# A hybrid attention and S5 layer on one core: gate spills moved to ScalarE's queue, own buffers for scaled u, output transposes and gate tiles moved in the state-space loop, the attention gate scaled ahead of its product

## Chip, cores and metric

The kernel runs on one core of a Trainium2 chip. Its engines are TensorE (PE), VectorE (V, in the trace DVE), ScalarE (A, ACT), GpSimd (Q, POOL) and SyncE (SP), which only issues DMAs here. The metric is the device time of one execution in microseconds, the median of the runs.

## What is computed

One layer over 1024 tokens of width 1024, in float32:

```python
xn = rms_norm(h, mix_norm)
q, k, v, gate_a, u, gate_s = split(xn @ w_in)          # 512 columns each
attn = dilated_mixture_attention(q, k, v, q_norm, k_norm) * silu(gate_a)   # 8 heads of 64
ssm  = s5_glu(u, ...) * silu(gate_s)                   # 32 groups of 16 channels, 64 complex states
h = h + concat(attn, ssm) @ w_out
h = h + sigmoid(rms_norm(h, ple_norm) @ w_ple_gate) * (p @ w_ple_proj)
```

The state-space part is a linear recurrence per group, `x[t] = a x[t-1] + B u[t]`, `y = Re(C x) + D u`, then a GELU and a gated linear unit.

## The kernel before

Each large product is made of three passes on PE (`mm3`): both factors are split into a high part and a residue, written `wh`, `wl` and `xh`, `xl`. A weight tile of 128 by 512 comes by DMA into one of three raw buffers (`wr`), ScalarE makes `wh` of it (L177), and POOL or VectorE the residue `wl` (L178). A tile of the gates takes 24 matmuls.

The order of the work is the Tile scheduler's: every engine and SP's DMA queue has its own in-order list of instructions, sorted by program order, by the priorities that `tc.high_priority` gives, and by a simulated timeline. While `T.held` is true, PE's instructions stay in the order in which the program writes them; that is so from the first gate tiles to the end of the state-space loop. The q, k, v products behind it are free again.

The stages that the change touches:

- **u and its scaling.** First u is computed for all tokens (tile by tile into PSUM, copied by ScalarE to `uraw`, L243 and L251). The gate tiles need the two "big" banks that the last copies of u (L251) free. `stats_rows` (L204) makes the row factor `rrow`. Then L496 to L507 multiply u by `rrow` on POOL (e = 0) and VectorE (e = 1) into eight tiles `ust`, which SP stores to `u_s` in DRAM; `ssm_inputs` loads them back as `ut` in another layout. The `ust` tiles come from `ev`, a ring of four buffers, which the gate tiles (`gate_a`, `gate_s`) use too. The pool `s2`, which holds the scan's tiles, is opened after the pool of `uraw` is closed (L509, L510) and lies over its memory.
- **The gates.** `gates()` (L282) is a generator: one step computes a tile of the attention gate (eight tiles, the first two together, so seven steps) or of the state-space gate (eight steps), applies SiLU on ScalarE, and SP stores it to `sa_s` or `sg_s` (L289, L299). `fill(n)` takes n steps. There is one step before the parameters, three at L495, one between `kern_pe(0)` and `kern_pe(1)`, one in each iteration of the loop, and one more in iterations 0 and 1 (L685). So the loop has a gate tile in iterations 0 to 7.
- **The parameters.** VectorE works out the powers of the recurrence (`pa`, `pb`, `mcs`, `msn`); four of their rows are copied by ScalarE at L487 to L490.
- **The state-space loop** has nine iterations, for half u blocks i = 0 to 7. Iteration i does on PE: `scan_pe(i)` (vp), `fill`, `ssm_out(i-1)` (yp), in iterations 2, 4, 6, 8 `ssm_store` (yt: transposes of the gelu of yp, which ScalarE makes at L643), and `kern_pe(i+2)` (gp, a transpose of the kernel `g`, and kp). Beside it VectorE and POOL do the scan (L613 to L625), the kernel of i + 2 (`kern_build`) and the tables of i + 1 (`table`). gp and yt use the "t" banks, of which there are two; ScalarE copies yt out at L653 (yo) and gp at L553. The scan's scratch tiles are in a ring of `SB[7]` buffers.
- **Attention** (L795) runs block by block, woven into the v, GLU and output products by `step(n)`. For each head: scores, row minimum, exp, split into f16 halves (L846 to L851), a transposing DMA to `pt`, and pv, which is summed in the one "pv" bank. Then pv is multiplied by the factor of the softmax sum, `dn` (L876). `output(b)` (L798) loads the gate tile into one buffer, POOL multiplies by it (L802), and PE transposes the product. The outputs of blocks 0, 1, 4 and 5 are held back to a later block.

Of the kernel before, what the change touches and what calls it, by code (L numbers as in the profile page):

```python
# [10 lines left out]
F32 = mybir.dt.float32  # L11
# [4 lines left out]
OP = mybir.AluOpType  # L16
# [41 lines left out]
VG = ((0, 1), (2,), (3,), (4,), (5,), (6,), (7,))  # L58
OS = (2,) * 8 + (3,) * 8
PB = {"prb": (2, 2), "hl": (2, 2), "pt": (3, 2)}  # L60
SB = (2, 1, 1, 1, 4, 4, 4, 8)
P = 128
S = 1024
D = 1024
# [17 lines left out]
def hybrid_layer(ctx: ExitStack, tc: tile.TileContext, a: dict, dbg=None):  # L82
# [199 lines left out]
    def gates():  # L282
        w = [load_w(wp, a["w_in"], k, 1536, lo=GLA) for k in range(KT)]
        for bs in ((0, 1), (2,), (3,), (4,), (5,), (6,), (7,)):
            for b, o in zip(bs, tok_tiles(w, bs, [f"ga{b}" for b in bs], "big")):
                gt_ = ev(f"gate_a{b}")
                with tc.high_priority(offset=AHEAD):
                    A.activation(gt_, o, AF.Silu, scale=rcol[:, b:b + 1])
                nc.sync.dma_start(sa_s[b], gt_)  # L289
            yield  # L290
        w = [load_w(wp, a["w_in"], k, 2560, lo=GL) for k in range(KT)]
        for f in range(4):
            for n in range(2):
                o = feat_tile(w, f, n, "big", f"gs{f}{n}")
                gt_ = ev(f"gate_s{f}{n}")
                with tc.high_priority(offset=AHEAD):
                    V.tensor_tensor(gt_, o, rrow[:, n * 512:(n + 1) * 512], op=OP.mult)
                    A.activation(gt_, gt_, AF.Silu)
                nc.sync.dma_start(sg_s[f * P:(f + 1) * P, n * 512:(n + 1) * 512], gt_)  # L299
                yield  # L300

    gates_ = gates()
# [181 lines left out]
    for j, m in enumerate((1, 2, 4)):  # L484
        turned(va[:, :, 0:m], vb[:, :, 0:m], va[:, :, m:2 * m], vb[:, :, m:2 * m], 3 * j, 3, [P, 3, m, G])
    turned(*(x[:, a_:a_ + 8].unsqueeze(1) for a_ in (18, 26) for x in (pa, pb)), 10, 1, [P, 1, 8, G])
    A.activation(pa[0:64, 8], mcs[0:64, 9], AF.Copy)  # L487
    A.activation(pa[64:128, 8], msn[64:128, 9], AF.Copy, scale=-1.0)
    A.activation(pb[0:64, 8], msn[0:64, 9], AF.Copy, scale=-1.0)
    A.activation(pb[64:128, 8], mcs[64:128, 9], AF.Copy, scale=-1.0)  # L490

    def rows(x, i, n, gs):
        return x[:, i:i + n, gs].rearrange("p i g -> p g i")

    fill(3)  # L495
    for f in range(4):  # L496
        ust = [ev(f"ust{f}{e}", (P, 4, P)) for e in range(2)]
        for n in range(2):
            o = uraw[f][:, n * 512:(n + 1) * 512]
            v5 = "p (b c e h) -> p e c b h"  # L500
            ov, rv = (t_.rearrange(v5, b=4, c=4, e=2) for t_ in (o, rrow[:, n * 512:(n + 1) * 512]))
            for e in range(2):
              with tc.high_priority(offset=AHEAD):
                E[UE[e]].tensor_tensor(ust[e][:, :, n * 64:(n + 1) * 64].rearrange("p c (b h) -> p c b h", b=4),
                                ov[:, e], rv[:, e], op=OP.mult)
        for e in range(2):
            nc.sync.dma_start(u_s[f, 4 * e:4 * e + 4].rearrange("j p k -> p j k"), ust[e])  # L507
# [151 lines left out]
    gcp = {i: kern_build(i) for i in range(2)}  # L659
    tabs = {0: table(0)}  # L660
    inp = {0: ssm_inputs(0)}
    gt = {0: kern_pe(0, *gcp[0])}
    fill()
    gt[1] = kern_pe(1, *gcp[1])
    for i in range(9):
        if i < 8:
            f = i // 2
            if i % 2 == 0 and f < 3:
                inp[f + 1] = ssm_inputs(f + 1)
            vp3 = scan_pe(i, gt[i], inp[f])  # L670
        fill()
        if i < 8:
            xpv[i] = ssm_scan(i, vp3, *tabs[i], gcp[i][1])
        if i + 2 < 8:
            gcp[i + 2] = kern_build(i + 2)
        if i + 1 < 8:
            tabs[i + 1] = table(i + 1)
        if i:
            f, h2 = divmod(i - 1, 2)
            if not h2:  # L680
                ygt[f] = [wa(f"ygt{f}{e}", (P, 4, 8, 16)) for e in range(2)]
            ssm_out(f, h2, xpv[i - 1], ygt[f], gcp[i - 1][1], inp[f], wts[f])
            if h2:
                ssm_store(f, ygt[f])
        if i < 2:  # L685
            fill()
        if i + 2 < 8:
            gt[i + 2] = kern_pe(i + 2, *gcp[i + 2])
    fill(16)
    T.held = False  # L690
    sp.close()

    rrp.close()
# [101 lines left out]
    def attention():  # L795
        held = []

        def output(b):  # L798
            n, at_ = b // 4, atok.pop(b)
            gl = b3[0].tile([P, 4, P], F32, tag="ga", name=f"ga{b}", bufs=GA)  # L800
            nc.sync.dma_start(gl, sa_s[b].rearrange("p (r t) -> p r t", r=4))
            E[EA[b % 2]].tensor_tensor(at_, at_, gl, op=OP.mult)  # L802
            tp = bank("t", f"at{b}").rearrange("p (r t) -> p r t", t=P)
            for j in range(4):
                T.transpose(tp[:, j], at_[:, j], ident)
            if n not in ma:
                ma[n] = quad(f"mah{n}"), quad(f"mal{n}")
            split(*(t_[:, b % 4] for t_ in ma[n]), tp.rearrange("p r t -> p (r t)"), V)

        atok = {}  # L810
        for i_, b in enumerate(BO):
            k0, k1 = dense_kb[b]
            n, nf = k1 - k0, int(b >= 4)
# [6 lines left out]
            def row_min(hd, out, sc, msk, init, acc_):  # L820
                V.tensor_tensor_reduce(out, sc, msk, gm, init, op0=OP.add, op1=OP.min, accum_out=acc_[:, hd:hd + 1])  # L821

            for h0 in range(0, H, m):
                pr_ = buf("prb", f"p{b}{h0}", (P, 5, P))
                sc = bank("s", f"sc{b}{h0}")
                if b == 7 and h0 % 4 == 0:
                    far7 = bank(F7, f"far{b}{h0}")
                    for j in range(4):
                        far_scores(far7[:, j * P:(j + 1) * P], b, h0 + j)
                elif nf and b < 7:  # L830
                    far_scores(sc[:, n * P:nt * P], b, h0)
                for i in range(m):
                    for qq, st_ in ((qh, True), (ql, False)):
                        T.matmul(sc[:, i * n * P:(i + 1) * n * P], qq[:, h0 + i, b * P:(b + 1) * P],
                                 ks[:, h0 + i, k0 * P:k1 * P], start=st_, stop=not st_)
                if nf:
                    far = far7[:, h0 % 4 * P:(h0 % 4 + 1) * P] if b == 7 else sc[:, n * P:nt * P]
                    row_min(h0, pr_[:, 0], far, mfar(b), 3.3e38, mf)
                for i in range(m):
                    hc = slice(h0 + i, h0 + i + 1)  # L840
                    pb_ = pr_[:, i * nt:(i + 1) * nt]
                    row_min(h0 + i, pb_[:, nf:nt].rearrange("p a b -> p (a b)"), sc[:, i * n * P:(i + 1) * n * P],
                            mdense(n - 1, n), mf[:, hc] if nf else 3.3e38, mx)
                    A.activation(pb_, pb_, AF.Exp, bias=mx[:, hc], scale=-1.0, accum_out=dn[:, hc])  # L844
                na = m * nt
                hl = halves(f"hl{b}{h0}")  # L846
                if HE[b][h0 % len(HE[b])] == "A":
                    A.activation(hl[:, 0:na], pr_[:, 0:na], AF.Copy)  # L848
                else:
                    V.tensor_copy(hl[:, 0:na], pr_[:, 0:na])  # L850
                E[LE[b][h0 % len(LE[b])]].tensor_tensor(hl[:, na:2 * na], pr_[:, 0:na], hl[:, 0:na], op=OP.subtract)  # L851
                pt = buf("pt", f"pt{b}{h0}", (P, 10, P), F16)
                nc.sync.dma_start(pt[:, 0:2 * na], hl[:, 0:2 * na], transpose=True)
                for i in range(m):
                    hd = h0 + i
                    end = hd == H - 1
                    for j in range(n):
                        for lp, lv in ((0, 0), (0, 1), (1, 0)):
                            T.matmul(pv[:, hd], pt[:, nf + i * nt + j + na * lp, :], vv[:, k0 + j, hd, lv, :],
                                     start=first, stop=end and not nf and j == n - 1 and lp == 1)  # L860
                            first = False
                    if nf:
                        for lp, lv in ((0, 0), (0, 1), (1, 0)):
                            for c in range(4):
                                T.matmul(pv[32 * c:32 * c + 32, hd], pt[:, na * lp, 32 * c:32 * c + 32],
                                         vc[:, c, hd, lv, :], start=False, stop=end and lp == 1,
                                         tile_position=(0, 32 * c))
                if h0 + m < H:
                    yield
# [2 lines left out]
                    output(b_)  # L872
            V.reciprocal(dn, dn)
            ts(dn, dn, isv, OP.mult)
            atok[b] = wa(f"atok{b}", (P, 4, P))
            tt(atok[b].rearrange("p r (h d) -> p (r h) d", d=64), pv, dn.unsqueeze(2).to_broadcast([P, 8, 64]), OP.mult)  # L876
            if i_ not in HOLD:
                output(b)
            yield
# [288 lines left out]
```

## Time and profile before

| | us |
|---|---|
| median of 3 runs | 720.25 (720.01 to 724.09) |
| the profiled execution, its own time | 726.85 |
| its span, first to last instruction | 725.1 |
| PE busy in it | 652.3 (90%) |
| VectorE, POOL, ScalarE busy | 434.9, 302.0, 299.0 |

Times in the profile are microseconds from the start of the span. A busy time counts instructions in execution; waits show as idle time before an instruction, with the engine or DMA that ended them. The granted clock is the share of the 2.4 GHz that PE was given: 1 is 2.4 GHz, 0.5 is 1.2 GHz. An `SPq` line is an instruction of SP's DMA queue, a `DMA` line the transfer.

### The profile page before, as it was taken

The numbers are of one execution on the slowest core, as the hardware profiler recorded it, in microseconds if no ns is written. First come the engines' busy times: TensorE is split into PE (matmuls) and PEld (weight loads), VectorE is DVE, ScalarE is ACT, GpSimd is POOL, SyncE is SP. The second block draws the span as 40 slices with busy tenths as digits, with TensorE's granted clock in tenths as the row PEclk, the third lists the DMA queues.
The fourth block names the chain that finished last, engine by engine and source line by source line (L and its number), as shares of the span: only waits on it lengthen the run. The fifth ranks groups of instructions, "written<-read, shape, count | busy, mean of one in ns | idle before, by whom it ended". The sixth has DMA issues, their size and how long they took to land.

```text
span 725.1 us, 11010 instructions
## 1 busy us (share of the span) xinstructions
PE 652.3 (90%) x3964; PEld 515.3 (71%) x3964; DVE 434.9 (60%) x904; ACT 299.0 (41%) x571; POOL 302.0 (42%) x263
## 2 busy tenths in 40 slices
PE   8996938997977999999999789888989899999997
PEld 6874826786866988887767366655767688888786
DVE  5999347573632546767553999967823565726222
ACT  7533105455556523346643655634512455203110
POOL 3435046664744411524242874422411325543531
PEclk9998977998989899999999889989989899999999
DMA  7712161415061765853672886699866334113201
GB/s 258 219 43 74 45 183 42 144 66 101 23 103 42 135 82 88 195 95 90 165 128 61 204 184 142 167 203 202 167 170 205 127 117 131 59 59 122 81 29 59
DMA packets 155047, 87.26 MB, mean 120 GB/s; under 512 B 117232, under 2 KB 126320, under 8 KB 154992
## 3 DMA queue, kind: packets, MB, share of 16 engines
q1 hardware_dynamic: 154992, 86.56, 49.2%
q8 instruction: 31, 0.51, 0.3%
q14 instruction: 24, 0.20, 0.1%
HBM read 48.81 MB, written 17.27 MB: 91 GB/s over the span
## 4 chain that ended last, share of the span: by engine, by line
PE 60%; DMA 12%; DVE 12%; issue 5%; ACT 5%; POOL 5%; SPq 1%; DVEq 0%; ACTq 0%; POOLq 0%
PE gt L92 10%; PE ga L92 7%; PE q L92 6%; PE oa L92 6%; PE os L92 6%; PE k L92 5%; DMA pt<-hl 4%; PE gs L92 3%; PE pe L92 3%; DMA wr<-in_w_in 3%; PE v L92 2%; PE vp L92 2%; PE pv L92 2%; PE sc L92 2%; DMA wr<-in_w_out 1%
## 5 line engine op out<-in xcount | busy, mean ns | idle before, releaser
L178 POOL TENSOR_TENSOR wl<-wr,wh 128x512 fp32r<-128x512 f32 x38 | 56.6, 1495 | 76.4 <-ACT wh L177 76.4
L177 ACT ACTIVATE wh<-wr 128x512 fp32r<-128x512 f32 x68 | 42.1, 627 | 61.6 <-DMA wr<-in_w_in 21.8
L851 POOL TENSOR_TENSOR hl<-p,hl 128x384 f16<-128x384 f32 (+2 forms) x34 | 40.5, 1195 | 63.3 <-ACT hl L848 29.1
L844 ACT ACTIVATE p<-p,st 128x384 f32<-128x384 f32 (+4 forms) x64 | 39.9, 623 | 54.6 <-DVE st L821 54.4
L92 PE MATMUL gt<-hh,wh 128*128 128x512 f32 (+1 forms) x136 | 51.8, 383 | 0.0
L92 PE MATMUL gt<-hl,wh 128*128 128x512 f32 (+1 forms) x136 | 51.7, 382 | 0.0
L92 PE MATMUL gt<-hh,wl 128*128 128x512 f32 (+1 forms) x136 | 51.2, 383 | 0.0
L92 PEld LDWEIGHTS <-pt 128*128 128x128 f16 (+1 forms) x888 | 26.7, 101 | 24.9 <-DMA pt<-hl 13.9
L178 DVE TENSOR_TENSOR wl<-wr,wh 128x512 fp32r<-128x512 f32 x30 | 26.3, 877 | 28.9 <-ACT wh L177 26.6
L1058 ACT ACTIVATE gg<-gg 128x512 f32<-128x512 f32 (+1 forms) x17 | 10.1, 605 | 66.5 <-DVE gg L361 66.3
L1060 POOL TENSOR_TENSOR gg<-gg,hs 128x512 f32<-128x512 f32 x14 | 18.0, 1290 | 41.7 <-DVE gg L361 40.1
L92 PE MATMUL pv<-vv,pt 128*128 128x64 f16 x504 | 25.5, 202 | 10.8 <-DMA pt<-hl 9.9
L92 PE MATMUL ga<-wh,xh 128*128 128x512 f32 x64 | 27.4, 428 | 6.7 <-ACT uraw L251 6.7
L92 PE MATMUL sc<-ks,qh 128*32 128x128 f16 (+4 forms) x160 | 24.8, 272 | 6.5 <-DVE st L821 6.3
L361 DVE TENSOR_TENSOR gg<-gt,rrow 128x512 f32<-128x512 f32 (+1 forms) x17 | 10.7, 655 | 32.7 <-PE gt L92 32.6
L850 DVE CAST hl<-p 128x384 f16<-128x384 f32 (+2 forms) x34 | 20.2, 597 | 16.5 <-DMA pt<-hl 12.0
L92 PE MATMUL os<-msh,wh 128*128 128x512 f32 x64 | 27.9, 435 | 2.3 <-DVE xos L372 2.3
L92 PEld LDWEIGHTS gt<-hh,wh 128*128 128x128 f32 x136 | 25.6, 188 | 5.6 <-ACT wh L180 0.3
L92 PE MATMUL oa<-mah,wh 128*128 128x512 f32 x64 | 26.7, 416 | 3.2 <-DVE xoa L372 3.2
L92 PEld LDWEIGHTS gt<-hh,wl 128*128 128x128 f32 x136 | 25.6, 188 | 5.4
L92 PEld LDWEIGHTS gt<-hl,wh 128*128 128x128 f32 x136 | 25.6, 188 | 5.4
L1013 POOL TENSOR_TENSOR ssb<-ssb,xoa 128x512 f32<-128x512 f32 x12 | 16.0, 1333 | 30.0 <-ACT xoa L1012 30.0
(303 smaller groups left out, 2015.2 us busy)
## 6 DMA issues: line engine op xcount, KB each, us to landing
wr<-in_w_in SPq DMA_DIRECT2D x48, 256.0 KB, 3.0
xr<-in_x SPq DMA_DIRECT2D x16, 256.0 KB, 4.7
wr<-in_w_out SPq DMA_DIRECT2D x16, 256.0 KB, 3.5
xos<-in_x SPq DMA_DIRECT2D x16, 256.0 KB, 3.6
h_s<-xos SPq DMA_DIRECT2D x16, 256.0 KB, 3.7
xoa<-h_s SPq DMA_DIRECT2D x16, 256.0 KB, 2.7
wr<-in_w_ple_gate SPq DMA_DIRECT2D x16, 256.0 KB, 3.1
out_t<-gg SPq DMA_DIRECT2D x15, 256.0 KB, 2.1
```

What stands on the lines that cost most here:

```text
L92: i = nc.tensor.matmul(*args, **kw)
L177: A.activation(hi, raw, AF.Copy)
L178: E[lo_on[k % len(lo_on)]].tensor_tensor(lo, raw, hi.bitcast(F32), op=OP.subtract)
L361: V.tensor_tensor(o, x, y, op=op)
L844: A.activation(pb_, pb_, AF.Exp, bias=mx[:, hc], scale=-1.0, accum_out=dn[:, hc])
L850: V.tensor_copy(hl[:, 0:na], pr_[:, 0:na])
L851: E[LE[b][h0 % len(LE[b])]].tensor_tensor(hl[:, na:2 * na], pr_[:, 0:na], hl[:, 0:na], op=OP.subtract)
L1013: E[SB2[f]].tensor_tensor(ssb[:, c], ssb[:, c], xr, op=OP.add)
L1058: A.activation(gt_, gt_, AF.Sigmoid)
L1060: (V if last else Q).tensor_tensor(gt_, gt_, hs, op=OP.add)
```

## The change

1. The gate tiles' stores to `sa_s` and `sg_s` are issued on ScalarE's queue, at the priority of the SiLU ahead of them, no longer on SP's.
2. The `ust` tiles get three buffers of their own; the scan's scratch ring shrinks from eight to six.
3. The four copies into `pa` and `pb` are done by VectorE, no longer by ScalarE.
4. Two more steps of the gates go ahead of `kern_pe(0)`, and the second step of iteration 1 is dropped. The 15 steps of the gates then end in iteration 6; iterations 7 and 8 have none.
5. `ssm_store` moves from iterations 2, 4, 6, 8 to iterations 3, 5, 7 and behind the loop, where PE's order is free.
6. In attention the gate tile of a block is loaded at the block's start, from the pool `b2` instead of `b3`; POOL multiplies it by `dn`, and VectorE multiplies pv by that product. `output(b)` has no multiplication left.
7. The scratch for dynamic DMAs is 512 instead of 1024.

```diff
-SB = (2, 1, 1, 1, 4, 4, 4, 8)
+SB = (2, 1, 1, 1, 4, 4, 4, 6)
...
                 with tc.high_priority(offset=AHEAD):
                     A.activation(gt_, o, AF.Silu, scale=rcol[:, b:b + 1])
-                nc.sync.dma_start(sa_s[b], gt_)
+                    A.dma_start(sa_s[b], gt_)
...
                     A.activation(gt_, gt_, AF.Silu)
-                nc.sync.dma_start(sg_s[f * P:(f + 1) * P, n * 512:(n + 1) * 512], gt_)
+                    A.dma_start(sg_s[f * P:(f + 1) * P, n * 512:(n + 1) * 512], gt_)
...
-    A.activation(pa[0:64, 8], mcs[0:64, 9], AF.Copy)
-    A.activation(pa[64:128, 8], msn[64:128, 9], AF.Copy, scale=-1.0)
-    A.activation(pb[0:64, 8], msn[0:64, 9], AF.Copy, scale=-1.0)
-    A.activation(pb[64:128, 8], mcs[64:128, 9], AF.Copy, scale=-1.0)
+    ts(pa[0:64, 8], mcs[0:64, 9], 1.0, OP.mult)
+    ts(pa[64:128, 8], msn[64:128, 9], -1.0, OP.mult)
+    ts(pb[0:64, 8], msn[0:64, 9], -1.0, OP.mult)
+    ts(pb[64:128, 8], mcs[64:128, 9], -1.0, OP.mult)
...
-        ust = [ev(f"ust{f}{e}", (P, 4, P)) for e in range(2)]
+        ust = [s1.tile([P, 4, P], F32, tag="ust", name=f"ust{f}{e}", bufs=3) for e in range(2)]
...
     inp = {0: ssm_inputs(0)}
+    fill(2)
     gt = {0: kern_pe(0, *gcp[0])}
...
             ssm_out(f, h2, xpv[i - 1], ygt[f], gcp[i - 1][1], inp[f], wts[f])
-            if h2:
-                ssm_store(f, ygt[f])
-        if i < 2:
+        if i and i % 2 == 1 and i > 1:
+            ssm_store(i // 2 - 1, ygt[i // 2 - 1])
+        if i < 1:
             fill()
...
     fill(16)
     T.held = False
+    ssm_store(3, ygt[3])
...
         def output(b):
             n, at_ = b // 4, atok.pop(b)
-            gl = b3[0].tile([P, 4, P], F32, tag="ga", name=f"ga{b}", bufs=GA)
-            nc.sync.dma_start(gl, sa_s[b].rearrange("p (r t) -> p r t", r=4))
-            E[EA[b % 2]].tensor_tensor(at_, at_, gl, op=OP.mult)
...
+            gates_of[b] = b2t("ga", f"ga{b}", (P, 8, 64), GA)
+            nc.sync.dma_start(gates_of[b].rearrange("p h d -> p (h d)"), sa_s[b])
             for h0 in range(0, H, m):
...
             ts(dn, dn, isv, OP.mult)
+            gl = gates_of.pop(b)
+            Q.tensor_tensor(gl, gl, dn.unsqueeze(2).to_broadcast([P, 8, 64]), op=OP.mult)
             atok[b] = wa(f"atok{b}", (P, 4, P))
-            tt(atok[b].rearrange("p r (h d) -> p (r h) d", d=64), pv, dn.unsqueeze(2).to_broadcast([P, 8, 64]), OP.mult)
+            tt(atok[b].rearrange("p r (h d) -> p (r h) d", d=64), pv, gl, OP.mult)
...
-    nc = bacc.Bacc("TRN2", target_bir_lowering=False, num_devices=1, dynamic_dma_scratch_size=1024)
+    nc = bacc.Bacc("TRN2", target_bir_lowering=False, num_devices=1, dynamic_dma_scratch_size=512)
```

## Rows read from the trace of the kernel before

**Rows 1.** The span and the mean granted clock of the core.

```profile
core 0: 725.1 us, clock 0.938
```

**Rows 2.** Busy time of each engine in three stretches; columns: stretch and its length, busy us and instructions of PE, of PE's weight loads, VectorE (DVE), ScalarE (ACT) and GpSimd (POOL), then the granted clock, the DMA engines' busy share and GB/s.

```profile
100.00:120.00 20.00, 9.14 (x33) 7.26 (x34) 15.87 (x13) 5.29 (x15) 17.34 (x13) 0.58 0.46 137
180.00:200.00 20.00, 18.47 (x118) 16.08 (x116) 13.79 (x22) 9.41 (x18) 14.67 (x14) 1.00 0.07 24
260.00:300.00 40.00, 40.00 (x172) 32.15 (x171) 25.29 (x63) 13.93 (x20) 11.95 (x9) 1.00 0.61 97
```

**Rows 3.** Whom PE waited for; columns: us in total, times, longest.

```profile
PE yt L98 <- ACT ygt L643: 13.2, 3, 4.9
PE gp L98 <- issue: 12.2, 1, 12.2
...
PE ga L92 <- ACT uraw L251: 6.7, 1, 6.7
...
PE kp L92 <- DVE cp L539: 2.5, 1, 2.5
...
PE gp L98 <- ACT yo L653: 0.8, 1, 0.8
```

**Rows 4.** Timeline of ScalarE, 48 to 66 us; columns: start, length, instruction, in brackets the idle time before it and what ended it.

```profile
56.95 0.23 ACT L488 ACTIVATE pa<-msn 64x32 f32<-64x32 f32 x1 [6.69 <-DVE msn L361]
...
62.40 0.63 ACT L177 ACTIVATE wh<-wr 128x512 fp32r<-128x512 f32 x1 [2.89 <-DMA wr<-in_w_in]
62.94 1.07 ACT L251 ACTIVATE uraw<-u 128x512 f32<-128x512 f32 x2
```

**Rows 5.** Timeline of POOL, 40 to 125 us.

```profile
63.73 5.10 POOL L178 TENSOR_TENSOR wl<-wr,wh 128x512 fp32r<-128x512 f32 x3
...
93.45 1.42 POOL L504 TENSOR_TENSOR ust<-uraw,rrow 128x256 f32<-128x256 f32 x2 [11.60 <-DMA sa_s<-gate_a]
...
104.13 1.61 POOL L532 TENSOR_TENSOR g<-pa,ba 128x512 f32<-128x512 f32 x1 [0.76 <-DVE ust L504]
```

**Rows 6.** Timeline of SP's DMA issues, 20 to 260 us; the length of several merged issues holds the waits between them.

```profile
49.09 20.10 SPq L172 DMA_DIRECT2D wr<-in_w_in  x8
77.54 19.73 SPq L289 DMA_DIRECT2D sa_s<-gate_a  x5
97.37 7.00 SPq L507 DMA_DIRECT2D u_s<-ust  x8
```

**Rows 7.** DMA issues by transfer: count, KB each, median us from issue to landing.

```profile
wr<-in_w_in SPq DMA_DIRECT2D x48, 256.0 KB, 3.0
...
u_s<-ust SPq DMA_DIRECT2D x8, 256.0 KB, 2.7
...
pt<-hl SPq DMA_TRANSPOSE x54, 3.4
```

**Rows 8.** The chain of work that ended last, in order of time, from 35 to 82 and from 95 to 260 us; columns: start, us on the chain, what.

```profile
63.57 13.92 PE ga L92 x48
...
111.95 1.94 PE kp L92 x8
113.89 7.12 PE ga L92 x24
121.01 0.44 PE gp L98 x4
121.45 1.02 PE kp L92 x8
122.46 1.98 PE vp L92 x16
124.45 11.25 PE ga L92 x48
...
245.77 5.36 PE yp L92 x48
...
256.29 0.87 PE yt L98 x8
```

**Rows 9.** Timeline of PE, 160 to 240 us.

```profile
165.87 0.39 PE L92 MATMUL yp<-cpi,xpv 128*128 128x128 f32 x2
...
174.85 3.62 PE L92 MATMUL vp<-ut,gt 128*128 128x128 f32 x16
```

**Rows 10.** Instructions grouped by line, engine, operation and tile; columns: shapes, count, busy us, mean ns, idle time before them and what ended it.

```profile
L851 POOL TENSOR_TENSOR hl<-p,hl 128x384 f16<-128x384 f32 (+2 forms) x34 | 40.5, 1195 | 63.3 <-ACT hl L848 29.1 <-DVE hl L850 14.5 <-DVE vscale L366 6.0
L844 ACT ACTIVATE p<-p,st 128x384 f32<-128x384 f32 (+4 forms) x64 | 39.9, 623 | 54.6 <-DVE st L821 54.4
...
L625 POOL TENSOR_TENSOR xpv<-y,tf 128x508 f32<-128x508 f32 x8 | 20.5, 2568 | 13.4 <-DVE y L618 13.4
...
L802 POOL TENSOR_TENSOR atok<-atok,ga 128x512 f32<-128x512 f32 x8 | 10.9, 1358 | 26.0 <-DVE atok L361 24.2 <-DMA ga<-sa_s 1.9
```

**Rows 11.** Timeline of VectorE, 40 to 258 us.

```profile
78.42 0.69 DVE L210 COPY rrow<-st1r 128x512 f32<-128x512 f32 x1 [1.67 <-PE st1r L92]
...
159.78 1.67 DVE L533 TENSOR_TENSOR gw<-pb,bb 128x512 f32<-128x512 f32 x1
...
196.42 0.68 DVE L533 TENSOR_TENSOR gw<-pb,bb 128x512 f32<-128x512 f32 x1
```

**Rows 12.** What SP's DMA issues waited for; columns: us in total, times, longest.

```profile
SPq L801 <- POOL atok L802: 4.3, 5, 1.8
```

More of the change, by code (lines that the diff above doesn't have):

```diff
@@ L808, in output @@
             split(*(t_[:, b % 4] for t_ in ma[n]), tp.rearrange("p r t -> p (r t)"), V)
-        atok = {}
+        atok, gates_of = {}, {}
         for i_, b in enumerate(BO):
```

## Prediction

> **What bounds the kernel now.** I read the mean clock first [rows 1], then the busy times in stretches [rows 2], then who TensorE (PE) waited for [rows 3], and last the engines' timelines around each of those waits. PE is the bound in most stages, so the question in each is where it stands still or runs at 1.2 instead of 2.4 GHz. Nearly all of what can be won lies before 257 us. Between 260 and 300 us, in q and k, PE is busy all the time at full clock; from 100 to 120 us it is busy 9.14 of 20 us at a granted clock of 0.58 [rows 2]. Five rows of PE's waits are touched by the change: 13.2 us (yt for the gelu), 12.2 and 2.5 us (gp and kp, the kernel build), 6.7 us (the first gate tiles for the copies of u) and 0.8 us (gp for yo) [rows 3]. Each also costs the slow clock behind it: a gate tile of 24 matmuls took 7.12 us behind the long wait, and two tiles 11.25 us, 5.62 each, a little later [rows 8].
>
> **A, four small copies from ScalarE to VectorE.** ScalarE's queue is in order. Its copy of `msn` into `pa` waited 6.69 us for VectorE, until 56.95 us, and stood ahead of four weight conversions and of the copies of u that free PE's banks (62.94 us) [rows 4]. Without it, as if the order stays: the fourth gate weight was asked for at 49.09 us [rows 6] and is there 3.0 us later [rows 7], at 52.1; conversion 0.63 [rows 4] and POOL's residue, at most 1.7 (5.10 for three) [rows 5], free its raw buffer at 54.4. The seventh weight lands at 57.4, is converted at 58.0, and the first copy of u (0.54) lets PE begin at 58.6 instead of 63.6: 5.0 us. The first pair of tiles then ran 13.92 us [rows 8], partly slow. At full clock it would be 11.25, but POOL's last three residues end at 63.73 + 5.10 = 68.8 us [rows 5] and wait for VectorE, not for ScalarE, half a us later behind the four copies, so the last weight's eighth of the pair (1.4) ends it near 70.7, against 77.5: 6.8. The bounds are 5 (slow again) and 8 (POOL moves up too). I take **6.5**. The four copies cost VectorE a few tenths each, in a stretch that ends well before anyone needs it.
>
> **B, own buffers for the scaled u, and two gate tiles ahead of the first kernel.** The `ust` tiles share four buffers with the gate tiles, so a product waits until a gate tile has been computed, stored and landed: POOL's second pair began at 93.45 us after 11.60 us of waiting for such a store [rows 5], and SP spent 77.5 to 97.3 us on five stores before the first u store [rows 6]. The kernel build starts only when the last `ust` is done, at 104.13 us [rows 5], since its pool lies over the memory of u. With three buffers of its own the first products start with the row factors. These waited 1.67 us for PE at 78.42 us, so VectorE's own work before them ends at 76.8 [rows 11]; with A PE is earlier than that, and with the four copies and one factor (0.69) the start is near 78 us. Eight tiles go round three buffers: product 1.4 for two halves [rows 5], issue 0.88 (7.00 for eight) [rows 6], landing 2.7 [rows 7], 5.0 a round, two rounds and a last product: 78 + 10 + 1.4, the end at about 89 us. PE needs cp 7.8 us after that (104.13 to 111.95 now, [rows 5, 8]), at 97. PE itself reached gp at 111.95 - 2.5 - 0.9 (gp at the slow clock, twice 0.44 [rows 8]) - 12.2 = 96.4 us; 6.5 earlier (A), and with two more tiles of 5.62 ahead of it, that is 101.1. So the build is there 4 us before it is needed, and the whole loss goes: 12.2 + 2.5 of waiting, 1.94 - 1.02 = 0.9 in kp and 7.12 - 5.62 = 1.5 in the next tile [rows 8]: **17.1**. The cover is those two tiles; without them 101.1 would be 89.9 and PE would wait 7 us again. They are taken from the end of the loop (below, D).
>
> **C, the transposes of the output an iteration later.** One stall worked out: yp ends at 165.87 + 0.39 = 166.3 us, the next vp at 174.85 + 3.62 = 178.5 [rows 9], 12.2 us. The work in it at full clock is yt 0.87, gp 0.44, kp 1.02, vp 1.98 [rows 8], 4.3. So 7.9 is lost, of it 4.5 waiting and 3.4 slow clock. Three stalls wait 13.2 + 0.8 = 14.0 us [rows 3]; the last one has no gp and kp behind it, so I count two and a half times 3.4: **22.5** in all. The transposes then read a gelu result that is an iteration old, and this wait can't come back. What is late next: gp follows yt on PE's fixed order and takes one of the two "t" banks, which yo's copy on ScalarE must free first. In the program gelu stands ahead of yo, so ScalarE may take it first. Two iterations have yt and gp (the third has no gp any more). Below, nothing; above, as much as now, 7.9 each. It cost 0.8 of waiting when ScalarE was early [rows 3]. I take 4.5 each: **-9**. The gelu of the next u block needs the buffers that yt reads, one PE step later: nothing.
>
> **D, the tail.** The last two iterations have no gate tile. Between vp and yp of the last one PE has yp (5.36 for two, 2.7 [rows 8]) and yt; the rest of the scan's way, some 4 us, may be filled by q's matmuls, whose order is free. Already now q runs ahead of the last yt. 0 to 7.5 with slow clock; I take **-1**. The number of tiles is the same, and PE's sum is too.
>
> **E, what I cost at nothing.** Spills issued by ScalarE: 16 issues of about 0.33 us, the length of SP's, beside an engine busy half of that time; SP no longer holds loads behind a gate that isn't done, but none of these is what PE waits for in [rows 3]. Six instead of eight scratch tiles: six are alive at most (two xpv of the last step, y, two new ones, ew). If the slot of an xpv frees only with yp, the chain starts up to 3 us later under 9 us of PE work. The gate's product in attention stays one POOL instruction per block, 1358 ns [rows 10], ahead of the read of pv and not behind it. Its factor is known when the last head's exponentials are, before the split, the transposing DMA and pv (1.20 [rows 10] and 3.4 [rows 7] alone), so it hides; the loads ahead of time take off at most 1.9 us of POOL's waiting [rows 10]. 0 to 2.7 (two products); I take 0.
>
> **Sum.** 6.5 + 17.1 + 22.5 - 9 - 1 = 36.1 us. It is made against the profiled execution (span 725.1, its own time 726.85 us), where it leaves 689.0 of span. The runs shown have a median of 720.25, 6.6 below that execution; I take the same microseconds off it: **684 us**.
>
> **Rivals.**
> 1. No new stall: yo is early, the tail is filled. 46.1 us, 674 us. For it: the bank's wait is the smallest of the five now [rows 3]. Against: gelu and yo become ready together, and gelu stands first in the program. 0.17.
> 2. The stall moves whole from yt to gp's bank, twice 7.9, and the tail is bare (7.5): 46.1 - 23.3 = 22.8, **697 us**. For it: 0.8 was seen there. Against: only the queue's order can bring 7.9. 0.17.
> 3. Without PE's waits the vector engines set the pace of the loop. POOL waits 13.4 us for the scan over eight steps [rows 10]; if that comes onto PE's path, 36.1 - 13.4 gives 697.5. Against: from 180 to 200 us PE was busy 18.47 of 20, POOL 14.67, VectorE 13.79 [rows 2], so all three fit. For it: the same gw product took 0.68 us alone and 1.67 beside POOL [rows 11]. The Trainium skill's page SBUF — State Buffer, section "Who interferes with whom", says that a VectorE instruction with two SBUF inputs and a GpSimd instruction that reads SBUF hold one shared port in turn, the later one standing still; the trace agrees (1.67 against 0.68), and by it a denser loop collides more. 0.08.
> 4. The buffers don't bring u forward (its stores are late for another reason): PE comes at 101.1 and waits until 108.5 as now, 7.4, and slow clock, 2.4, is back: 26.3, **694 us**. 0.07.
> 5. Slower: the gate load of the next block stands on SP's queue ahead of the probabilities' transposing DMAs, and has one buffer, free only after the last block's product. If SP issues it first, each of seven blocks starts its first head anew: product 1.36, exp 0.62, residue 1.20 [rows 10], transposing DMA 3.4 [rows 7], 6.6 each, 46 in all: 730 us. It decides from 36.1 / 7 = 5.2 us a block. Against: this load has the same single buffer now and held SP 4.3 us in five waits, 1.8 at most [rows 12]. 0.05.
>
> **Numbers.** My forecast, 679 to 690, has 0.46. The range goes to rival 1 with the upper ends of A and E (669) and beyond rivals 2 to 4 with the lower end of A and a little of two at once (702). One per cent, 7 us, is about what this kernel's runs can tell from no change. All cases but rival 5 are faster by more, save two of rivals 2 to 4 together (some 0.04, near 713): faster 0.91, same 0.04, slower 0.05.
>
> **What would show it.** A: PE's first gate tile before 60 us. B: no wait of gp or kp, the last `ust` near 89 us, clock at 1 from 100 to 120. C: no wait of yt for gelu; a wait of gp for yo of some 3 us, twice. D: q's matmuls between the last vp and yp. End of the loop 36 us earlier, and the same distance from q to the end. It is wrong if ScalarE's order puts something new ahead of u's copies, if yo lies far back in its queue, or if attention grows by more than 5 us.

## The result, and the profile after

| | median | range | profiled execution (span) | granted clock |
|---|---|---|---|---|
| before | 720.13 us (4 runs) | 719.91 to 724.09 | 726.85 (725.1) | 0.938 |
| changed | 696.50 us (4 runs) | 694.86 to 701.35 | 701.35 (699.6) | 0.961 |

The ratio is 0.967, with a 95% interval of 0.961 to 0.973: faster by 23.6 us. Between the two profiled executions it is 25.5 us. The time lies inside the range, 12.5 us above the forecast and half a microsecond from rival 2, so the steps matter more than the sum.

PE's waits, answering to [rows 3] (columns: total, times, longest):

```profile
PE gp L98 <- ACT yo L653: 13.9, 2, 8.6
...
PE ga L92 <- ACT gate_a L288: 5.4, 1, 5.4
...
PE ga L92 <- ACT uraw L251: 1.2, 1, 1.2
```

The waits of yt for gelu and of gp and kp for the build are gone, and the gate tile's wait for u has fallen from 6.7 to 1.2 us. Two others stand where they were: gp waits 13.9 us for yo, and a gate tile waits 5.4 us for the SiLU of an earlier tile, which frees its bank.

ScalarE around the first gate tiles, answering to [rows 4]:

```profile
57.03 1.27 ACT L177 ACTIVATE wh<-wr 128x512 fp32r<-128x512 f32 x2 [2.29 <-PE u L92]
58.20 1.06 ACT L251 ACTIVATE uraw<-u 128x512 f32<-128x512 f32 x2
```

The wait for `msn` is out of the queue and the copies of u start at 58.20 instead of 62.94. PE's first gate tile starts at 58.84 (63.57 before), and the first pair ends at 71.64 (77.50): 5.9 us. The first spill on ScalarE's queue comes only behind it, at 71.70 us, so this gain is not the spills'.

SP's issues, answering to [rows 6]:

```profile
81.50 9.06 SPq L507 DMA_DIRECT2D u_s<-ust  x8
90.65 1.11 SPq L574 DMA_DIRECT2D ut<-u_s  x2
```

The last `ust` is done at 90.17 us; the prediction said 89. What happened to PE there is on ScalarE's timeline:

```profile
94.48 0.53 ACT L541 ACTIVATE bm<-g 128x16 f32<-128x16 f32 x4 [14.71 <-DVE g L534]
94.92 0.67 ACT L288 ACTIVATE gate_a<-ga,col 128x512 f32<-128x512 f32 x1
...
98.07 1.27 ACT L629 ACTIVATE cpi<-cp 64x512 f32<-64x512 f32 x2 [2.48 <-DVE cp L539]
99.36 0.69 ACT L288 ACTIVATE gate_a<-ga,col 128x512 f32<-128x512 f32 x1
```

`bm` is part of the kernel build. It stood ahead of the SiLU and waited 14.71 us for VectorE's g; the SiLU, whose input had been there since some 84.7 us, could start only at 94.92, and `cpi` did the same to the next one. On PE the tile waits 5.36 us, and gp of step 0 comes at 109.74 us:

```profile
95.64 0.79 PE L92 MATMUL ga<-wh,xh 128*128 128x512 f32 x1 [5.36 <-ACT gate_a L288]
...
109.74 0.60 PE L98 MATMUL gp<-ident,g 128*128 128x128 f32 x4
```

Busy times in stretches, answering to [rows 2]; the columns are those of that group:

```profile
80.00:100.00 20.00, 14.64 (x54) 11.38 (x54) 13.43 (x14) 3.00 (x8) 14.55 (x13) 0.87 0.59 185
100.00:120.00 20.00, 20.00 (x99) 16.11 (x98) 7.26 (x9) 9.24 (x20) 8.84 (x7) 0.96 0.24 81
```

From 100 to 120 us PE is busy throughout, at a clock of 0.96 (9.14 of 20 and 0.58 before). The hole has become smaller and lies one stretch earlier. When the same work is done (eight ga tiles, gp, kp and the first vp) the kernel before was at 135.7 us and the changed one at 120.6: 15.1 us, of which 5.9 are A's.

The second wait, on the chain of work that ended last (columns: start, us, what) and on PE:

```profile
167.30 1.29 DVE y L618 x4
...
169.22 2.08 DVE ew L594
171.31 0.61 DVE gate_s L297
171.94 0.64 ACT gate_s L298
172.60 0.33 ACTq L299
...
172.98 0.63 ACT tf L596
173.62 0.63 ACT tf L597
...
174.27 0.63 ACT cpi L629
174.91 0.63 ACT cpi L629
175.56 1.28 ACT L643
176.85 0.38 ACT ygt L643
177.23 0.50 ACT yo L653
...
238.56 2.68 PE yp L92 x24
```

```profile
168.16 1.04 PE L98 MATMUL yt<-ident,ygt 128*128 128x128 f32 x8
177.78 1.12 PE L98 MATMUL gp<-ident,g 128*128 128x128 f32 x4 [8.59 <-ACT yo L653]
178.82 1.97 PE L92 MATMUL kp<-cp,bm 128*64 128x128 f32 x8
```

The transposes are done at 169.2 us, but yo, which frees their bank, is the last of a row on ScalarE: the gate's SiLU (which waits for VectorE, behind the scan y and the product ew), the store of its tile, the two tf, the two cpi, the table load (line 643 without a tile), gelu, yo. With the slow clock behind each wait (kp takes 1.97 instead of 1.09 us) the two stalls cost 11.5 and 7.4 us, 18.9 in all. The loop's end (last yp, 241.2 us, less the 8.7 us of q's matmuls now inside; 251.1 before [rows 8]) is 18.6 us earlier than before, so the loop alone gave 3.5 of the 25.5. The stages behind it gave 6.9 more.

### The profile page after: what moved, and what is told of

Same layout as the page of the kernel before. It is cut to its first block, busy times and chain, and to the rows that moved or that the text cites. A ratio compares the mean times of both kernels' runs of the same rounds, so it can differ in the third digit from the quotient of the medians.

```text
span 699.6 us, 10983 instructions
## 1 busy us (share of the span) xinstructions
PE 642.5 (92%) x3964; PEld 508.9 (73%) x3964; DVE 450.1 (64%) x908; ACT 293.5 (42%) x565; POOL 292.7 (42%) x263
## 4 chain that ended last, share of the span: by engine, by line
PE 49%; DVE 21%; DMA 13%; POOL 5%; issue 5%; ACT 5%; SPq 1%; ACTq 0%; DVEq 0%; POOLq 0%
PE gt L92 10%; PE q L92 6%; PE oa L92 5%; PE k L92 5%; PE os L92 5%; DMA pt<-hl 4%; PE v L92 3%; PE pv L92 3%; PE pe L92 2%; DMA wr<-in_w_in 2%; PE glu L92 2%; PE sc L92 2%; PE ga L92 1%; DVE ew L594 1%; DVE wl L178 1%
## 5 line engine op out<-in xcount | busy, mean ns | idle before, releaser
L178 POOL TENSOR_TENSOR wl<-wr,wh 128x512 fp32r<-128x512 f32 x38 | 54.8, 1444 | 78.2 <-ACT wh L177 62.5
L178 DVE TENSOR_TENSOR wl<-wr,wh 128x512 fp32r<-128x512 f32 x30 | 28.0, 933 | 17.5 <-ACT wh L177 13.3
L820 DVE CUSTOM_DVE_ANT_0 p<-sc,mask,gc 128x128 f32<-128x128 f32 (+3 forms) x56 | 24.5, 458 | 8.0 <-PE sc L92 4.3
L851 DVE CAST hl<-p 128x384 f16<-128x384 f32 (+2 forms) x34 | 17.5, 521 | 16.9 <-DMA pt<-hl 8.2
L92 PE MATMUL ga<-wl,xh 128*128 128x512 f32 x64 | 26.8, 419 | 0.5 <-POOL wl L178 0.4
```

Source lines behind the costliest of these rows:

```text
L92: i = nc.tensor.matmul(*args, **kw)
L178: E[lo_on[k % len(lo_on)]].tensor_tensor(lo, raw, hi.bitcast(F32), op=OP.subtract)
```

## The experiments

Each ratio is against the kernel before on the same chip. "Against changed" is the difference from 0.967 in points, times 7.2 us; the changed kernel's own interval is 4 us to either side of that, so differences of 1 us are none, and those of 5 and 6 us lie at its edge. Within a group that shares one measurement of the kernel before, u_att lies 7 us above f_bm, and u_ust 7 above u_yt and u_tiles, clear of their intervals; f_gp lies 4 below f_bm, and there the intervals overlap.

| run | ratio, 95% interval | against changed |
|---|---|---|
| f_bm | 0.965 (0.962 to 0.969) | -1 |
| f_gp | 0.959 (0.955 to 0.964) | -5 |
| f_both | 0.961 (0.957 to 0.964) | -5 |
| u_att | 0.975 (0.972 to 0.979) | +6 |
| f_u2_sb7 | 0.966 (0.964 to 0.969) | -1 |
| f_noew | 0.958 (0.954 to 0.962) | -7 |
| f_early | 0.956 (0.953 to 0.959) | -8 |
| f_yt1 | 0.952 (0.949 to 0.955) | -11 |
| f_yt1_early | 0.938 (0.935 to 0.941) | -21 |
| u_yt | 0.966 (0.962 to 0.969) | -1 |
| u_ust | 0.975 (0.972 to 0.978) | +6 |
| u_tiles | 0.966 (0.963 to 0.970) | -1 |

Two theories for the missing gain (the letters are not engines). Q: two orders on ScalarE's queue, `bm` and `cpi` ahead of the SiLU, and yo behind the rest. P (rival 3): VectorE and POOL have become the loop's pace, and ScalarE is merely late with them.

**f_bm: the copies bm made by VectorE.**

```diff
-            A.activation(bm[h2][:, j, 16 * j:16 * j + 16], g[:, j, 0, :], AF.Copy)
+            ts(bm[h2][:, j, 16 * j:16 * j + 16], g[:, j, 0, :], 1.0, OP.mult)
```

> The changed kernel, with the four small copies into bm done by VectorE, so that they no longer stand on ScalarE's queue ahead of the SiLU of the fourth gate tile. Theory Q (the order of ScalarE's queue made both new waits): PE's wait of 5.4 us before the fifth gate tile goes, with about 2.8 us of slow clock behind it, 8 us in all: 688 us. Rival P (POOL and VectorE now set the pace of the state-space loop, and what PE gains ahead of it is lost in it): PE's wait goes, but the time falls by at most 3 us.

698.4 us, no gain. The wait moved one tile on: 5.7 us, now behind `cpi` alone. One of two blockers taken away is worth nothing.

```profile
PE ga L92 <- ACT gate_a L288: 5.7, 1, 5.7
```

```profile
101.37 1.27 ACT L629 ACTIVATE cpi<-cp 64x512 f32<-64x512 f32 x2 [14.14 <-DVE cp L539]
```

**f_gp: the output transposes behind kern_pe in the iteration; f_both: this and f_bm.**

```diff
-        if i and i % 2 == 1 and i > 1:
-            ssm_store(i // 2 - 1, ygt[i // 2 - 1])
...
             gt[i + 2] = kern_pe(i + 2, *gcp[i + 2])
+        if i and i % 2 == 1 and i > 1:
+            ssm_store(i // 2 - 1, ygt[i // 2 - 1])
```

> The changed kernel, with the output transposes behind gp and kp of the same iteration, so that gp no longer needs the bank that yo's copy frees. Theory Q: both waits of gp (8.6 and 5.3 us) go, with some 5 us of slow clock: 17 to 19 us less, about 679 us. Rival P: the same time is waited elsewhere in the loop, at vp, gp or yp for POOL and VectorE; at most 6 us less.

> Both edits together. Theory Q: 25 us less than the changed kernel, about 671 us, which is also where the prediction's case without any new stall stands (674). Rival P: 9 us less at most.

693.7 and 694.0 us: some 5 us gained, at the edge of what can be told apart, and far from Q's figures. PE's waits of f_gp show why: with the order turned round, the second transpose waits for the copy that empties gp's bank.

```profile
PE yt L98 <- ACT gt L553: 9.9, 2, 6.3
PE ga L92 <- ACT gate_a L288: 5.5, 1, 5.5
```

So far P looked better. But this order only exchanged one user of the "t" banks for the other.

**f_yt1: the transposes earlier, right behind the gate tile.** In PE's queue they then stand ahead of yp, in ScalarE's the first yo stands ahead of the table load for SiLU, and the second ahead of tf and gelu.

```diff
         fill()
+        if i and i % 2 == 1 and i > 1:
+            ssm_store(i // 2 - 1, ygt[i // 2 - 1])
         if i < 8:
             xpv[i] = ssm_scan(i, vp3, *tabs[i], gcp[i][1])
...
-        if i and i % 2 == 1 and i > 1:
-            ssm_store(i // 2 - 1, ygt[i // 2 - 1])
```

> The output transposes and their copies are given out still earlier in the iteration, right behind the gate tile: in PE's queue ahead of yp, in ScalarE's ahead of tf, the table load and gelu. The wait of gp for yo (13.9 us and 5 us of slow clock) then has no reason in either queue. Theory Q: the loop gains the whole 18.9 us less the 9 us that a step of PE's own work leaves, 679 to 683. Theory P: PE waits elsewhere instead (yp for xpv or cpi, vp for gt), and the time falls by at most 5 us, 691 to 696.

686.5 us. ScalarE's queue around the first yo, and PE's waits from 80 to 245 us:

```profile
165.53 0.60 ACT L653 ACTIVATE yo<-yt 128x512 f32<-128x512 f32 x1 [0.48 <-PE yt L98]
166.15 1.28 ACT L298 ACT_TABLE_LOAD   x1
...
171.92 0.59 ACT L653 ACTIVATE yo<-yt 128x512 f32<-128x512 f32 x1
```

```profile
PE ga L92 <- ACT gate_a L288: 5.5, 1, 5.5
PE q L92 <- DVE gate_s L297: 5.5, 1, 5.5
PE yt L98 <- ACT gt L553: 1.3, 1, 1.3
```

No wait of gp for yo is left, without a single engine's work having been cut. A step without transposes takes PE 11.7 us in both kernels; the first one with them, from the vp of iteration 3 to that of iteration 4, takes 12.6 us here (157.41 to 170.00) and took 22.7 in the changed kernel (157.99 to 180.72). What comes late next is the bank of the last gate tile, 5.5 us, which the earlier run of q's matmuls meets. This falls between the two theories' figures (Q 679 to 683, P 691 to 696) and, with f_early and f_yt1_early below, decides for Q.

**f_u2_sb7: ew ahead of xpv on VectorE again** (two buffers for the scaled u, so that seven scratch tiles fit).

```diff
-SB = (2, 1, 1, 1, 4, 4, 4, 6)
+SB = (2, 1, 1, 1, 4, 4, 4, 7)
...
-        ust = [s1.tile([P, 4, P], F32, tag="ust", name=f"ust{f}{e}", bufs=3) for e in range(2)]
+        ust = [s1.tile([P, 4, P], F32, tag="ust", name=f"ust{f}{e}", bufs=2) for e in range(2)]
```

> Two buffers for the reloaded u instead of three and seven scratch buffers instead of six. Its one difference in the loop is on VectorE: the product ew of the next table stands ahead of xpv again, as in the kernel before, and so does not run beside POOL's xpv. Theory P (the chain of VectorE and POOL sets the loop's pace, and ScalarE and PE wait for it): ew falls from 1.95 us to about 1.1, POOL's wait for ew (6.6 us in six steps) goes, the wait of gp for yo shrinks from 13.9 us to about 8, and the time falls by 5 to 8 us, to 689 to 691. Theory Q (only the places in ScalarE's and PE's queues matter): nothing on ScalarE or PE is moved in the loop, so 695 to 697.

The product ew got shorter, as P says; VectorE's group of it, 125 to 245 us, first in the changed kernel and then in this one:

```profile
L594 DVE TENSOR_TENSOR ew<-pb 128x512 f32<-128x512 f32 x7 | 12.8, 1824 | 0.0
```

```profile
L594 DVE TENSOR_TENSOR ew<-pb 128x512 f32<-128x512 f32 x7 | 7.4, 1054 | 0.0
```

The time stayed: 696.0 us, gp's wait 13.1 instead of 13.9. But the run did not make the pair of engines faster. POOL's xpv, in the changed kernel and then in this one, lost the 5 us that VectorE's ew had saved:

```profile
L625 POOL TENSOR_TENSOR xpv<-y,tf 128x508 f32<-128x508 f32 x8 | 14.6, 1820 | 13.6 <-DVE y L618 13.6
```

```profile
L625 POOL TENSOR_TENSOR xpv<-y,tf 128x508 f32<-128x508 f32 x8 | 19.8, 2477 | 14.1 <-DVE y L618 14.1
```

The two run beside each other in both kernels, and the one that starts later is the longer one. At the first stall POOL's xpv starts at 168.73 and takes 1.69 us, and ew, from 169.22, takes 2.08; here ew starts at 170.08 and takes 1.05, and xpv, from 170.30, takes 2.54. The table tc, for which ScalarE's tf waits, is ready 5.4 us after the scan y starts in the one and 5.3 us in the other. So the run is no test of P; it shows that it did not matter which of the two stood still. Nor is it a clean run: the two buffers made the build later, and the gate tile's wait grew from 5.4 to 8.8 us, which hides some 2 us that the loop gained (120.5 instead of 122.7 us from its first vp to its last yp). The Trainium skill's page SBUF — State Buffer, section "Who interferes with whom", says that a VectorE instruction with two inputs in SBUF and a GpSimd instruction that reads SBUF contend for one shared port, and that the order of issue decides which of them is blocked; the four durations agree with it.

**f_noew: the second product of the table and its subtraction left out in steps 1 to 7.**

```diff
-        w = q4("ew" + nm)
         Q.tensor_tensor(v4(tc_), hi_(pa), lo_(pa), op=OP.mult)
-        E[SE[4]].tensor_tensor(v4(w), hi_(pb), lo_(pb), op=OP.mult)
-        E[SE[5]].tensor_tensor(tc_, tc_, w, op=OP.subtract)
+        if i < 1:
+            w = q4("ew" + nm)
+            E[SE[4]].tensor_tensor(v4(w), hi_(pb), lo_(pb), op=OP.mult)
+            E[SE[5]].tensor_tensor(tc_, tc_, w, op=OP.subtract)
```

> Leaves out, for the tables of steps 1 to 7, the second product ew (VectorE, 1.95 us each) and its subtraction on POOL (1.33 us each): the tables of these steps hold their first product alone. Theory P: the chain of VectorE and POOL gets 2 to 3 us shorter in each of six steps, falls below PE's 11.7 us, the wait of gp for yo (13.9 us) falls under 4 and the loop ends 8 to 14 us earlier: 683 to 689. Theory Q: yo still stands behind the table load and gelu in ScalarE's queue, gp's wait stays, 693 to 697.

690.7 us, between the figures: gp's wait for yo fell from 13.9 to 7.5 us and no further.

```profile
PE gp L98 <- ACT yo L654: 7.5, 2, 4.1
```

The speed of the vector engines is a link of the chain shown above (ew stands ahead of the gate product that the SiLU waits for), but cutting it leaves more than half of the wait, while another place for yo takes it all.

**f_early: the build's first copies off ScalarE.**

```diff
         for j in range(4):
-            A.activation(bm[h2][:, j, 16 * j:16 * j + 16], g[:, j, 0, :], AF.Copy)
+            if i < 2:
+                ts(bm[h2][:, j, 16 * j:16 * j + 16], g[:, j, 0, :], 1.0, OP.mult)
+            else:
+                A.activation(bm[h2][:, j, 16 * j:16 * j + 16], g[:, j, 0, :], AF.Copy)
...
+        if i < 1:
+            for hf in range(2):
+                ts(cpi[64 * hf:64 * hf + 64], cpw[64:128, :, 1:9], 1.0, OP.mult)
+            ts(cpw[64:128, :, 1:9], cpw[0:64, :, 1:9], 1.0, OP.mult)
+        else:
...
```

> The copies bm of steps 0 and 1 and cpi, cp of step 0 are made by VectorE, so that nothing of ScalarE's queue that waits for the build stands ahead of the SiLU of the attention gate tiles; the rest of the loop is as in the changed kernel. If the wait of 5.4 us and the slow clock behind it come from these two places, PE's wait for gate_a between 85 and 105 us goes and the transposes of gp for step 0 start near 102 us instead of 109.7. Theory Q: these 7 us reach the end, 689 to 690. Theory P: the vector engines begin their build no earlier, so the loop waits longer for them later and at most 3 us are left, 693 to 697.

688.3 us, as Q said. ScalarE now takes the SiLU at once, and PE's gp of step 0 comes at 103.17 instead of 109.74 us:

```profile
92.13 0.69 ACT L288 ACTIVATE gate_a<-ga,col 128x512 f32<-128x512 f32 x1 [4.93 <-PE ga L92]
```

```profile
103.17 0.60 PE L98 MATMUL gp<-ident,g 128*128 128x128 f32 x4
```

The 6.6 us reached the loop's end (7.3 there) and the time (8). What PE gains ahead of the loop is not lost again in it to the vector engines, as P would have it.

**f_yt1_early: both.**

> Both edits that helped, together: bm of steps 0 and 1 and cpi, cp of step 0 by VectorE, and the output transposes right behind the gate tile. Theory Q (two separate queue orders on ScalarE): their gains add, 8 and 10 us, 677 to 680. Theory P (once both are gone the vector engines set the pace): q's wait for the gate product, 5.5 us with the second edit alone, grows to 10 or more, 682 to 686.

680.3 us, ratio 0.938 (0.935 to 0.941): the gains of 8 and 11 add, to 21 in this measurement, and this version beats both kernels. The stretch from 130 to 200 us, the changed kernel and then this one:

```profile
130.00:200.00 70.00, 61.41 (x373) 53.34 (x372) 44.45 (x62) 38.69 (x78) 40.41 (x39) 0.93 0.32 69
```

```profile
130.00:200.00 70.00, 68.48 (x445) 59.96 (x444) 46.14 (x67) 44.25 (x83) 40.83 (x39) 1.00 0.32 71
```

PE fills 68.48 of 70 us at full clock, while VectorE has work for 46 and POOL for 41. P is refuted as the bound; f_noew left the vector engines a share in the stall, as a link of its chain. q's wait for the last gate product remains (5.4 us); it wasn't tried.

**u_yt, u_ust, u_tiles, u_att: one part taken back each.**

```diff
 u_yt:
+            if h2:
+                ssm_store(f, ygt[f])
-        if i and i % 2 == 1 and i > 1:
-            ssm_store(i // 2 - 1, ygt[i // 2 - 1])
...
-    ssm_store(3, ygt[3])
 u_ust:
-SB = (2, 1, 1, 1, 4, 4, 4, 6)
+SB = (2, 1, 1, 1, 4, 4, 4, 8)
-        ust = [s1.tile([P, 4, P], F32, tag="ust", name=f"ust{f}{e}", bufs=3) for e in range(2)]
+        ust = [ev(f"ust{f}{e}", (P, 4, P)) for e in range(2)]
 u_tiles:
-    fill(2)
     gt = {0: kern_pe(0, *gcp[0])}
...
-        if i < 1:
+        if i < 2:
             fill()
 u_att: the lines of the diff in attention, taken back
```

> The changed kernel with the output transposes where they were before, at the end of the step that makes their input; all else as changed. By the terms on record (22.5 us gained, 9 lost) the time rises by 13.5 to about 710. By the traces the loop itself gained 3.5 us, so about 700, with waits of yt for gelu of 3.7 to 4.9 us three times in place of the two waits of gp for yo.

699.5 us, ratio 0.966: no difference. The later transposes were worth nothing as made. Its longest waits, in place of gp's for yo:

```profile
PE yt L98 <- ACT ygt L643: 10.8, 2, 5.4
```

> The changed kernel with the reloaded u in the buffers of the gate again and eight scratch buffers. By the term on record (the reload comes 14 us earlier by its own buffers) the last ust lands near 100 us again, the build starts late and the time rises by 9 to 17, to 705 to 713. Rival: the spills on ScalarE's queue alone free the gate's buffers early enough, the last ust stays before 93 us and the time at 695 to 698.

706.3 us, ratio 0.975: 6 us slower than the changed kernel, less than the 9 expected. The buffers do bring u forward, as said; SP's issues end ten microseconds later without them:

```profile
84.96 15.29 SPq L507 DMA_DIRECT2D u_s<-ust  x8
```

> The changed kernel with the two gate tiles behind the first kp again. By the record (without them PE waits from 91 us to the build at 97 and takes 3 us more for the clock) the time rises by 7 to 10, to 704 to 707. By the trace of the changed kernel PE waits there for ScalarE anyway (5.4 us and 2.8 of slow clock), so the one wait takes the place of the other: 695 to 699, with a wait of gp for the build between 90 and 100 us and none of ga for gate_a.

701.1 us, ratio 0.966: no difference. Without the tiles PE waits for the build, and with them for ScalarE, which is held by the build; 4.9 us against 5.4:

```profile
PE kp L92 <- DVE cp L539: 2.6, 1, 2.6
PE gp L98 <- issue: 2.3, 1, 2.3
```

> The changed kernel with attention's gate as before: loaded in the output step, multiplied by POOL after pv. Theory: the 7 to 8 us that the stages behind q and k gained come from this part, so this kernel takes 702 to 705 us. Rival: they come from the other order of the schedule; within 2 us of the changed kernel, 695 to 699.

705.1 us, ratio 0.975: 6 us slower, as expected. The stages behind the loop gain this by the part in attention. One stretch of it, 530 to 550 us, the changed kernel and then u_att, where PE's first matmuls of the next stage wait 3.4 us for VectorE (0.9 in the changed kernel, 3.2 before):

```profile
530.00:550.00 20.00, 19.10 (x83) 15.13 (x82) 11.12 (x14) 7.45 (x13) 6.15 (x5) 1.00 0.55 174
```

```profile
530.00:550.00 20.00, 16.58 (x64) 12.74 (x63) 8.91 (x11) 6.70 (x11) 5.13 (x4) 0.91 0.59 183
```

## Why the prediction was right or wrong

The direction and the range were right. By the profiled executions A, B, C with D, and the stages behind the loop came out as 5.9 + 9.2 + 3.5 + 6.9 = 25.5 us, where the prediction had 6.5 + 17.1 + (13.5 - 1) + 0 = 36.1. That the time stayed inside the range is in part luck: B and C with D gave 16.9 us less than forecast, and the 6.9 us behind the loop were not forecast at all. By u_att, without the part in attention, the time would have stood at some 702 us, the upper end of the range.

- **A** was right: 5.9 for 6.5, and the first gate tile before 60 us. It is read from the trace alone; no run undid the copies, the spills or the smaller scratch for DMAs.
- **B, 17.1, gave 9.2.** The times up to the build were met: u at 90.17 for 89, and `cp` at 98.0 for 97, with no wait of gp or kp. PE's own arrival at gp was not: 109.7 for 101.1. The step that failed is "the build is there 4 us before it is needed, and the whole loss goes". It asked when the build is ready for PE, and not who else waits for the build: its copies on ScalarE stand ahead of the SiLU that frees the bank of the very tiles that were to cover the time. f_early, where PE is at gp at 103.2, shows the missing 7 to 8 us there. "The cover is those two tiles" was wrong as it stood (u_tiles).
- **C, 22.5 less 9, gave 3.5.** The first number was met, since yt's waits all went. The second was mis-sized: 18.9 instead of 9, more even than the upper bound of 15.8. That bound assumed yo right behind gelu, as in [rows 3]; ahead of the two stood the gate's SiLU, tf, cpi and a table load too. The prediction named this as what would make it wrong ("if yo lies far back in its queue"); the trace of before, which shows the old order alone, could not say. With yo placed first (f_yt1) the part gave 11 us more, some 14 in all.
- **D** was right: q's matmuls lie between the last vp and yp, and 0.4 us of waiting is left.
- **E, the attention's gate, bounded 0 to 2.7 and taken as 0,** gave 6. The prediction priced POOL's product, and not what waits for the output behind it. In u_att PE waits 2.5 us longer for the next stage's input than in the changed kernel; what carries the rest of the 6 us was not taken apart.
- **Rivals.** Rival 2 gave the time (697) and half of the mechanism: the stall did move whole to gp's bank, 13.9 us for 13.2, but the tail was not bare, and B and E were off by about as much (7.9 and 6.9) in opposite directions; that its time was met is luck. Rival 3 is refuted as a bound by f_yt1_early, though f_noew shows that ew and its subtraction carry almost half of the wait for yo. Its reading of [rows 11] was wrong: the gw of 0.68 us, at 196.42, was not alone but ran beside POOL's xpv (195.66 to 198.83 us), which took 3.17 us where it takes 1.69 in the changed kernel, there ahead of ew. So beside each other one of the two is slow, and it need not be VectorE. Rival 4 is refuted by the trace. Rival 5 did not show.

The parts taken back one by one (6 for the buffers, 6 for attention, 0 for the tiles and the transposes) and A's 6 make 18 of the 23.6 us. The rest is not assigned: the tiles and the transposes cover for other parts, and no two were undone together.

## What to carry to other kernels

When a matmul waits for an instruction on an in-order engine, list everything that stands ahead of that instruction in its queue and what each of those waits for; the time at which its own input is ready is not enough. Moving work out of one wait often only makes it the next one in line (yt for gelu, gp for yo, yt for gt were three faces of one stall), so the move to look for is the one that puts the instruction that frees a bank first in its queue. And take away all blockers of a queue at once before judging: one of two gave 1 us, both gave 8.

## What the runs showed of the hardware

A DMA issue on ScalarE's queue took 0.33 us. Where its data had long been there, it did not hold the next instruction: the issue at 102.08 us ran while tf was being made from 102.02 on, and the second tf followed at 102.66. Right behind the SiLU whose result it stores it did: in the chain above it runs from 172.60 to 172.93, and tf, whose tc was there at 172.65, follows at 172.98. The spills, which the prediction had at nothing, cost some 0.3 us there.

```profile
102.02 0.63 ACT L596 ACTIVATE tf<-tc 64x512 f32<-64x512 f32 x1 [1.97 <-POOL tc L595]
102.08 0.33 ACTq L289 DMA_DIRECT2D sa_s<-gate_a  x1
102.66 0.63 ACT L597 ACTIVATE tf<-tc 64x512 f32<-64x512 f32 x1
```
